# Encoder layer on one core: first gate weights loaded behind the first four x tiles, seven of the first head's weight subtractions on VectorE, two later norms issued one round sooner

## The chip, the cores and the metric

The kernel runs on one core of a Trainium2 chip. The metric is the device time of one execution in microseconds. Five engines matter here: TensorE (PE in the profile, with its weight loads as PEld), VectorE (DVE), ScalarE (ACT), GpSimd (POOL) and SyncE (SP), which issues most of the DMA transfers. Each engine executes its own instructions strictly in the order of its queue, and waits on semaphores where an instruction needs the result of another engine or of a transfer.

## What is computed

One residual encoder layer on x of 1024 positions by 1024 channels, in float32. Cut to what matters:

```python
h = rmsnorm(x, g_mix)
z = h @ w_in                      # columns: pooling channels | q | k | v
y_pool = pool_mixer(u_pool, w_pool_grp, pool_scale)
y_attn = diff_attention(q, k, v, g_q, g_k, lam, g_sub, lambda_init)   # 8 heads
gates = sigmoid(h @ w_gate + b_gate)
merged = gates[..., :1024] * (y_pool @ w_branch_pool) + gates[..., 1024:] * (y_attn @ w_branch_attn)
x = x + merged @ w_out
x = x + square(relu(rmsnorm(x, g_ffn) @ w_up)) @ w_down
```

## The kernel before

**Products.** A float32 operand is split into two parts: ScalarE copies it rounded (`hi`, a CAST row), and VectorE or GpSimd subtracts that from the source (`lo`, a TENSOR_TENSOR row). A product is then three matmuls into one PSUM bank, hi by hi, hi by lo and lo by hi (`mm3`, L138 to L140), so the third or the second of them waits for a subtraction. Weights and the normed, transposed h are both split in this way.

**The start of the program.** SyncE loads x0 (two halves), the first half of the first head's weights (`rqkv0_0`, `rqkv0_1`, each holding two of the eight k tiles), x1, the other half, two small rows, then x2 and x3. The list of instructions from there to the norm of x2 is written out by hand, and `q` (L423 to L432) chains every one of them behind the one before it on its engine, so that all of them carry the line L432. x0 and x1 are normed on ScalarE (Square with a sum), VectorE and GpSimd (a power of -0.5), scaled on VectorE (`hn`), transposed on TensorE into PSUM banks `hps`, and split into `hT`. `split_k(k)` splits weight tile k of the first head: ScalarE makes `hi`, and `POOL_W` lists the tiles whose `lo` GpSimd makes, VectorE making the others.

**The rounds.** After that a loop over rounds g issues stages of work for head h and position tile t (g = 8h + t): `A` is the q, k, v product `z` of one tile (24 matmuls of 384 columns into one of two PSUM banks of the pool `ps_z`), `B` its norm (`qn` on VectorE is the last reader of a `z` bank), `C` transposes q and k (`tk`), `D` the scores, and so on. x4 to x7 are loaded in rounds 0 and 1 (`LX`) and normed (`norm_x`, with `norm_transpose`, L282 and L287) in the rounds that `NX` lists. The norms of x1 to x7 there stand in `issue_after(h_hi[t - 2].ins)`: the norm's ScalarE instructions are queued behind the last `hi` copy of x(t-2). `issue_after` acts only on instructions of the engine of the one that it names.

**Fillers.** From round 5 on, half a unit a round, gate columns are computed between these stages: `gate_cols(c)` loads 128 columns of `w_gate` in two tiles (`frgate`, 256 KB each), splits them (`fwgate`, the subtraction on GpSimd) and multiplies them with the two halves of hT (`g`, 24 matmuls of 512 columns for each half of the positions).

**What sets the order.** The rounds give each instruction a priority; a scheduler then puts the instructions of each engine into a fixed order before the program runs, by its own estimate of when an operand is there. So an edit at one place can move instructions of all engines for some while after it. Here the order of all engines is the same again, row by row, from about the 1370th of TensorE's 7262 rows on.

Of the kernel before, what the change touches and what calls it, by code (L numbers as in the profile page):

```python
# [17 lines left out]
P = 128  # L18
# [19 lines left out]
N_QKVW = 8 * H  # L38


NX = [-9, -9, -9, -9, 2, 3, 3, 4]
LX = [-2, -2, -2, -2, 0, 0, 1, 1]
FU = 170
N_W1, N_W2 = 9, 16
POOL_W = (0,3,4,6)
G_DIST, G_COLS = 3, 2

O = "B1 C2 H7 D4 R8 E5 F6 W-2 A0"
# [15 lines left out]
def encoder_kernel(  # L64
# [21 lines left out]
    nc = tc.nc  # L86
    x, out = x[0], out[0]
# [69 lines left out]
    def fo_tile(name):  # L157
        return fp.tile([P, 528], F32, tag="fo", name=name, bufs=N_FO)
# [29 lines left out]
    loads = {}  # L188
# [103 lines left out]

    h_hi = {}

    def alloc_T(tile_fn, prefix, th):
        return {
            (kp, th, hl): tile_fn([P, 2, 512], F32R, f"{prefix}{kp}_{th}_{hl}", th)
            for kp in range(NK // 2)
            for hl in range(2)
        }  # L300
# [73 lines left out]
            nc.scalar.dma_start(p_dram[g * P : (g + 1) * P, th * 512 : (th + 1) * 512], yp[:, 0:512])  # L374

    def gate_cols(c):
        with tc.issue_after(h_hi[c + 2].ins) if c < 3 else nullcontext():
            ws = fill_w(w_gate, c * P, f"gate{c}")
        for th in range(2):
            ps = fill_proj(ws, th, f"g{c}_{th}", spare_bank if c >= G_Z else fill_bank)  # L380
            fo = fo_tile(f"go{c}_{th}")
            nc.scalar.activation(fo[:, 0:512], ps, AF.Identity, bias=cols[:, c : c + 1])  # L382
            nc.scalar.dma_start(g_dram[c * P : (c + 1) * P, th * 512 : (th + 1) * 512], fo[:, 0:512])
            yield
# [23 lines left out]
    with ExitStack() as ph:  # L408
# [8 lines left out]
        xs = {}  # L417
# [3 lines left out]
        @contextmanager  # L421
        def behind():
            with ExitStack() as stack:  # L423
                for ins in queued.values():
                    stack.enter_context(tc.issue_after(ins))
                yield

        def q(make, *args, **kw):
            if not in_turn[0]:
                return make(*args, **kw)  # L430
            with behind():
                done = make(*args, **kw)  # L432
            queued[done.ins.engine] = done.ins
            return done
# [9 lines left out]
        def load_x(t):  # L444
            xs[t] = htile([P, D], F32, f"x{t}", 1) if t < 2 else ut([P, D], F32, f"x{t}")
            for c in range(0, D, 512 if t < 2 else D):
                e = c + 512 if t < 2 else D
                q(nc.sync.dma_start, xs[t][:, c:e], x[t * P : (t + 1) * P, c:e])

        w_qkv = w_in[:, POOLD:].rearrange("(kk p) (s c) -> p kk s c", p=P, s=3)  # L450
        Wh = {}
# [94 lines left out]
        def turn(t, j):  # L546
            xt, hn, ss, s1_, rs = row[t]
            js = halves[j]
            if t == 0 and j == 0:
                q(act.activation, hn[:, js], hn[:, js], AF.Copy, scale=rs)  # L550
            else:
                q(dve.scalar_tensor_tensor, hn[:, js], xt[:, js], rs, gmb[:, js], op0=ALU.mult, op1=ALU.mult)
            pool_, tag = [(ps_t, "tr"), (ps_s, "sc")][j]
            ps = pool_.tile([P, 512], F32, tag=tag, name=f"hps{t}_{j}")
            for i in range(4):
                k = 4 * j + i
                go = q if t == 0 else lambda make, *args: make(*args)
                go(nc.tensor.transpose, ps[:, i * P : (i + 1) * P], hn[:, k * P : (k + 1) * P], identf)
            return ps
# [7 lines left out]
        def split_k(k, hi=True):  # L567
            if hi:
                Wh.setdefault(0, []).append(wt([P, 2, 384], f"wqkv0_{k}"))
            w, src = Wh[0][k], raws[0, k // 2][:, k % 2, :]  # L570
            if hi:
                q(act.copy, w[:, 0, :], src)
            if k or not hi:
                q((pol if k in POOL_W else dve).tensor_tensor, w[:, 1, :], src, f(w[:, 0, :]), op=ALU.subtract)

# [25 lines left out]
        split_h(0, 2, h0[1])  # L601
        scale_1()
        split_k(5)
        h1 = [turn(1, 0)]
        split_h(0, 3, h0[1])
        split_k(6)
        split_k(7)
        split_h(1, 0, h1[0])
        h1.append(turn(1, 1))
# [303 lines left out]
        for g in range(-2, N + 10):  # L913
            for t in range(4, NT):
                if LX[t] == g:
                    load_x(t)
            for t in range(1, NT):
                if NX[t] == g:
                    with tc.issue_after(h_hi[t - 2].ins):
                        norm_x(t)  # L920
            if g == G_DIST:
                with behind():
                    distances()
            if g == G_COLS:
                columns()
            gens = {}
            for tok in ORDER:
                if tok not in gens:
                    i = g - tok[1]
                    gens[tok] = stage(tok[0], i) if 0 <= i < N else iter(())  # L930
                next(gens[tok], None)
            for gen in gens.values():
                for _ in gen:
                    pass
            while made < F_UNITS and made < (g - F_FROM) * F_PACE:
                next(units)
                made += 1
# [82 lines left out]
    for d in range(NK):  # L1020
# [17 lines left out]
        if d >= 4:  # L1038
            e = d - 4
# [176 lines left out]
    for step in O_TAIL.split():  # L1216
        t = int(step[1])
# [396 lines left out]
```

## Time and profile before

| | us |
|---|---|
| median of three runs | 1532.42 (1532.18 to 1532.62) |
| the profiled execution's own time | 1534.07 |
| its span, first to last instruction | 1532.3 |
| TensorE busy in the span | 1518.9 |
| VectorE, ScalarE, GpSimd busy | 1023.4, 795.2, 393.9 |
| mean granted TensorE clock | 0.998 |

In a row of the timeline the first number is the start in us from the span's first instruction and the second the duration, then engine, source line, operation and tiles (buffer numbers left out), and in brackets the idle time of the engine before it with what ended that. "x4" is four such rows merged; "out<-in" names tiles by the program.

### The profile page before, as it was taken

The numbers are of one execution on the slowest core, as the hardware profiler recorded it, in microseconds if no ns is written. First come the engines' busy times: TensorE is split into PE (matmuls) and PEld (weight loads), VectorE is DVE, ScalarE is ACT, GpSimd is POOL, SyncE is SP. The second block draws the span as 40 slices with busy tenths as digits, with TensorE's granted clock in tenths as the row PEclk, the third lists the DMA queues.
The fourth block names the chain that finished last, engine by engine and source line by source line (L and its number), as shares of the span: only waits on it lengthen the run. The fifth ranks groups of instructions, "written<-read, shape, count | busy, mean of one in ns | idle before, by whom it ended". The sixth has DMA issues, their size and how long they took to land.

```text
span 1532.3 us, 21742 instructions
## 1 busy us (share of the span) xinstructions
PE 1518.9 (99%) x7637; PEld 1317.4 (86%) x7637; DVE 1023.4 (67%) x2132; ACT 795.2 (52%) x1653; POOL 393.9 (26%) x469
## 2 busy tenths in 40 slices
PE   8999999999999999999999999999999999999998
PEld 7899999999999999888888887888888788888887
DVE  7776767677777777742745898676656678556572
ACT  5755555555555555644633467565555634333331
POOL 5524242434334352318646510000000000000000
PEclk9999999999999999999999999999999999999999
DMA  6211111111202021339745633555433899537650
GB/s 211 64 38 58 47 56 56 58 49 40 73 30 80 30 90 49 117 104 375 266 141 185 203 135 117 172 183 167 152 124 110 289 328 365 186 125 261 230 189 28
DMA packets 168584, 213.75 MB, mean 139 GB/s; under 512 B 10166, under 2 KB 104091, under 8 KB 168475
## 3 DMA queue, kind: packets, MB, share of 16 engines
q1 hardware_dynamic: 151050, 185.05, 35.9%
q10 hardware_dynamic: 17424, 27.31, 4.8%
q8 instruction: 60, 0.98, 0.3%
q14 instruction: 50, 0.40, 0.1%
HBM read 154.62 MB, written 57.70 MB: 139 GB/s over the span
## 4 chain that ended last, share of the span: by engine, by line
PE 92%; DVE 5%; issue 1%; ACT 1%; DMA 0%; POOL 0%; POOLq 0%; SPq 0%; ACTq 0%; DVEq 0%
PE z L140 5%; PE z L139 5%; PE z L138 5%; PE Da L139 4%; PE Da L140 4%; PE g L139 4%; PE Da L138 4%; PE g L140 4%; PE g L138 4%; PE Db L140 3%; PE Db L139 3%; PE Db L138 3%; PE X L138 3%; PE X L140 3%; PE X L139 3%; PE sc L763 2%
## 5 line engine op out<-in xcount | busy, mean ns | idle before, releaser
L138 PE MATMUL z<-wqkv,hT 128*128 128x384 f32 x512 | 173.9, 340 | 0.3 <-DVE qn L699 0.3
L139 PE MATMUL z<-wqkv,hT 128*128 128x384 f32 x512 | 173.6, 339 | 0.5 <-POOL wqkv L432 0.5
L140 PE MATMUL z<-wqkv,hT 128*128 128x384 f32 x512 | 173.2, 339 | 0.2 <-DVE hT L430 0.2
L773 ACT ACTIVATE s<-s,nm 128x256 f32<-128x256 f32 (+7 forms) x128 | 99.6, 778 | 80.0 <-DVE nm L765 77.0
L271 POOL TENSOR_TENSOR ms<-ms,mhalf 128x4 f32<-128x4 f32 x64 | 66.9, 1045 | 200.1 <-DVE ms L270 196.6
L138 PE MATMUL g<-hT,fwgate 128*128 128x512 f32 x256 | 101.1, 395 | 0.0
L139 PE MATMUL g<-hT,fwgate 128*128 128x512 f32 x256 | 100.6, 393 | 0.2 <-DVE hT L132 0.2
L140 PE MATMUL g<-hT,fwgate 128*128 128x512 f32 x256 | 100.2, 392 | 0.0
L138 PEld LDWEIGHTS z<-wqkv,hT 128*128 128x128 f32 x512 | 96.2, 188 | 3.0 <-DVE qn L699 0.5
L139 PEld LDWEIGHTS z<-wqkv,hT 128*128 128x128 f32 x512 | 96.3, 188 | 2.7 <-POOL wqkv L432 0.8
L140 PEld LDWEIGHTS z<-wqkv,hT 128*128 128x128 f32 x512 | 96.2, 188 | 2.0 <-DVE hT L430 0.7
L765 DVE CUSTOM_DVE_ANT_0 s<-sc,dist 128x512 f32<-128x512 f32 (+3 forms) x128 | 74.4, 585 | 21.7 <-PE sc L763 21.0
L762 PE MATMUL sc<-K,Q 128*128 128x512 f32 (+2 forms) x192 | 67.6, 357 | 0.4 <-DVE nm L765 0.4
L763 PE MATMUL sc<-K,Q 128*128 128x512 f32 (+2 forms) x192 | 66.3, 349 | 0.0
L132 DVE TENSOR_TENSOR AS<-s,AS 128x512 fp32r<-128x512 f32 x64 | 43.5, 688 | 32.9 <-ACT AS L131 32.9
L132 POOL TENSOR_TENSOR wqkv<-rqkv,wqkv 128x384 fp32r<-128x384 f32 x56 | 58.6, 1059 | 13.7 <-ACT wqkv L131 12.2
L132 POOL TENSOR_TENSOR fwgate<-frgate,fwgate 128x512 fp32r<-128x512 f32 x32 | 43.6, 1366 | 58.6 <-ACT fwgate L131 58.6
L140 PEld LDWEIGHTS g<-hT,fwgate 128*128 128x128 f32 x256 | 48.1, 188 | 9.5
L139 PEld LDWEIGHTS g<-hT,fwgate 128*128 128x128 f32 x256 | 48.1, 188 | 9.3 <-DVE hT L132 0.6
L138 PEld LDWEIGHTS g<-hT,fwgate 128*128 128x128 f32 x256 | 48.1, 188 | 9.1 <-ACT go L382 0.2
L138 PE MATMUL ba<-yT,wba 128*128 128x512 f32 x128 | 49.6, 389 | 0.0
L139 PE MATMUL ba<-yT,wba 128*128 128x512 f32 x128 | 49.6, 389 | 0.0
(481 smaller groups left out, 4613.0 us busy)
## 6 DMA issues: line engine op xcount, KB each, us to landing
wd<-in_w_down_dram SPq DMA_DIRECT2D x56, 512.0 KB, 5.9
wu<-in_w_up_dram SPq DMA_DIRECT2D x32, 512.0 KB, 4.6
udS<-us SPq DMA_DIRECT2D x64, 256.0 KB, 3.5
ur<-udS SPq DMA_DIRECT2D x32, 512.0 KB, 4.4
rqkv<-in_w_in_dram SPq DMA_DIRECT2D x64, 192.0 KB, 3.4
ur<-ud SPq DMA_DIRECT2D x24, 512.0 KB, 6.0
frgate<-in_w_gate_dram SPq DMA_DIRECT2D x32, 256.0 KB, 2.7
g_dram<-go ACTq DMA_DIRECT2D x32, 256.0 KB, 3.0
```

The lines of the kernel that those rows point to most:

```text
L132: (lo_eng or nc.vector).tensor_tensor(lo, src, f(hi), op=ALU.subtract)
L138: nc.tensor.matmul(ps, lhs_hi, rhs_hi, start=first, stop=False, **kw)
L139: nc.tensor.matmul(ps, lhs_hi, rhs_lo, start=False, stop=False, **kw)
L140: return nc.tensor.matmul(ps, lhs_lo, rhs_hi, start=False, stop=last, **kw)
L271: nc.gpsimd.tensor_tensor(dst, dst, mhalf[:, :n], op=ALU.pow)
L762: nc.tensor.matmul(dst, Q[:, i, 0, :], rhs, start=True, stop=False)
L763: nc.tensor.matmul(dst, Q[:, i, 1, :], rhs, start=False, stop=True)
L765: nc.vector.tensor_tensor_reduce(out=s[i][:, c : c + w], in0=sc[:, 0:w], in1=dist[:, o0 + c : o0 + c + w], scale=2.0 ** -(h + 1), scalar=B ...
L773: nc.scalar.activation(s[i][:, 0:n], s[i][:, 0:n], AF.Exp, bias=last, scale=-1.0, accum_out=Z[:, i, t : t + 1])
```

## The change

Three things are edited. The loads of the first three gate columns get a second `issue_after`, behind the load of x3 on SyncE's queue; before, their only one named a ScalarE instruction and did not hold the loads. `POOL_W` shrinks from tiles 0, 3, 4, 6 to tile 3, and the split of weight tile 6 stands ahead of the scaling of x1 in the written list. The norms of x5 and x7 are issued in rounds 2 and 3 in place of 3 and 4, and the norms of x6 and x7 lose their `issue_after`.

```diff
-NX = [-9, -9, -9, -9, 2, 3, 3, 4]
+NX = [-9, -9, -9, -9, 2, 2, 3, 3]
-POOL_W = (0,3,4,6)
+POOL_W = (3,)
...
+    @contextmanager
+    def first_gates(c):
+        with tc.issue_after(h_hi[c + 2].ins), tc.issue_after(loads["x3"].ins):
+            yield
...
     def gate_cols(c):
-        with tc.issue_after(h_hi[c + 2].ins) if c < 3 else nullcontext():
+        with first_gates(c) if c < 3 else nullcontext():
...
-                q(nc.sync.dma_start, xs[t][:, c:e], x[t * P : (t + 1) * P, c:e])
+                loads[f"x{t}"] = q(nc.sync.dma_start, xs[t][:, c:e], x[t * P : (t + 1) * P, c:e])
...
         split_k(5)
+        split_k(6)
         h1 = [turn(1, 0)]
         split_h(0, 3, h0[1])
-        split_k(6)
         split_k(7)
...
-                    with tc.issue_after(h_hi[t - 2].ins):
+                    with tc.issue_after(h_hi[t - 2].ins) if t < 6 else nullcontext():
                         norm_x(t)
```

In the rows below the number behind a tile's name is its index in the program (`x0`, `hn5`, `frgate0_0`: first tile of gate column 0; `wqkv0_4`: head 0, weight tile 4; `z0_2`: head 0, position tile 2; `hps4_1`: second transposed half of x4; `g0_1`: gate column 0, second half of the positions), and the last number is a serial one. Source lines below L300 keep their numbers, later ones move by five.

SyncE, the first transfers that it issues, before:

```order
L307 DMA frgate0_0_789<-in_w_gate_dram 128x4x128
L432 DMA x0_145<-in_x_dram 128x512 x2
L432 DMA rqkv0_0_148<-in_w_in_dram 128x3x128 x2
L432 DMA rqkv0_1_151<-in_w_in_dram 128x3x128 x2
L432 DMA x1_154<-in_x_dram 128x512 x2
```

And the changed kernel's rows 13 to 18 of SyncE, behind x2, x3 and the small rows:

```order
L437 DMA rows_357<-in_g_sub_dram 1x128
L437 DMA rows_357<-in_g_ffn_dram 8x128
L437 DMA lqk_363<-in_lambda_qk_dram 128x256
L312 DMA frgate0_0_789<-in_w_gate_dram 128x4x128
L312 DMA frgate0_1_794<-in_w_gate_dram 128x4x128
L435 DMA rqkv1_0_850<-in_w_in_dram 128x3x128 x2
```

The first gate tile went from the head of the queue to the place just ahead of the second gate tile; the changed queue begins with x0.

VectorE, from the scaling of x0 to the sum of squares of x1, before:

```order
L432 SCALAR_TENSOR_TENSOR hn0_192<-x0_145,rsa0_195,gmb_179 128x512
L432 TENSOR_TENSOR wqkv0_1_246<-rqkv0_0_148,wqkv0_1_246 128x384
L432 TENSOR_TENSOR hT0_0_1_172<-hps0_0_234,hT0_0_0_171 128x2x128
L432 TENSOR_TENSOR wqkv0_2_251<-rqkv0_1_151,wqkv0_2_251 128x384
L432 TENSOR_TENSOR hT1_0_1_174<-hps0_0_234,hT1_0_0_173 128x2x128
L432 ISA hn1_262,ssb1_264<-x1_154 128x512
```

and now:

```order
L437 SCALAR_TENSOR_TENSOR hn0_192<-x0_145,rsa0_195,gmb_179 128x512
L437 TENSOR_TENSOR wqkv0_0_231<-rqkv0_0_148,wqkv0_0_231 128x384
L437 TENSOR_TENSOR wqkv0_1_246<-rqkv0_0_148,wqkv0_1_246 128x384
L437 TENSOR_TENSOR hT0_0_1_172<-hps0_0_234,hT0_0_0_171 128x2x128
L437 TENSOR_TENSOR wqkv0_2_251<-rqkv0_1_151,wqkv0_2_251 128x384
L437 TENSOR_TENSOR hT1_0_1_174<-hps0_0_234,hT1_0_0_173 128x2x128
L437 TENSOR_TENSOR wqkv0_4_259<-rqkv0_2_157,wqkv0_4_259 128x384
L437 ISA hn1_262,ssb1_264<-x1_154 128x512
```

Weight tiles 0 and 4 joined the queue here (and tile 6 further on, ahead of `hn1`).

VectorE again, ahead of `qn0_2`, the last reader of the PSUM bank that the product of position tile 4 takes next. Before:

```order
L695 TENSOR_REDUCE ms0_2_581<-sq0_2_580 128x4
L132 TENSOR_TENSOR V0_0_381<-z0_2_499,V0_0_381 128x128
L282 SCALAR_TENSOR_TENSOR hn5_524<-x5_375,rs5_526,gmb_179 128x512
L132 TENSOR_TENSOR hT0_1_1_451<-hps4_0_465,hT0_1_0_450 128x2x128
L282 SCALAR_TENSOR_TENSOR hn5_524<-x5_375,rs5_526,gmb_179 128x512
L270 TENSOR_SCALAR ms0_2_581<-ms0_2_581 128x4
L646 COPY cols_121<-cols_ps_484 128x32
L132 TENSOR_TENSOR hT1_1_1_453<-hps4_0_465,hT1_1_0_452 128x2x128
L647 TENSOR_SCALAR gs_122<-cols_121 128x1
L132 TENSOR_TENSOR hT2_1_1_455<-hps4_1_475,hT2_1_0_454 128x2x128
L132 TENSOR_TENSOR hT3_1_1_457<-hps4_1_475,hT3_1_0_456 128x2x128
L699 TENSOR_TENSOR qn0_2_588<-z0_2_499,ms0_2_581 128x256
```

and now:

```order
L700 TENSOR_REDUCE ms0_2_607<-sq0_2_606 128x4
L282 SCALAR_TENSOR_TENSOR hn5_484<-x5_375,rs5_486,gmb_179 128x512 x2
L132 TENSOR_TENSOR V0_0_381<-z0_2_525,V0_0_381 128x128
L132 TENSOR_TENSOR hT0_1_1_451<-hps4_0_465,hT0_1_0_450 128x2x128
L270 TENSOR_SCALAR ms0_2_607<-ms0_2_607 128x4
L282 SCALAR_TENSOR_TENSOR hn6_550<-x6_410,rs6_552,gmb_179 128x512 x2
L132 TENSOR_TENSOR hT1_1_1_453<-hps4_0_465,hT1_1_0_452 128x2x128
L700 TENSOR_REDUCE ms0_3_661<-sq0_3_660 128x4
L132 TENSOR_TENSOR V0_0_381<-z0_3_635,V0_0_381 128x128
L132 TENSOR_TENSOR hT2_1_1_455<-hps4_1_475,hT2_1_0_454 128x2x128
L270 TENSOR_SCALAR ms0_3_661<-ms0_3_661 128x4
L704 TENSOR_TENSOR qn0_2_614<-z0_2_525,ms0_2_607 128x256
```

Both halves of `hn6`, and two small steps of tile 3, now stand ahead of `qn0_2`. On ScalarE the Square of x6 likewise stands directly behind that of x5, ahead of the Square of `z0_2`.

TensorE, from the end of the product of tile 4 to the next work behind it. Before:

```order
L138 MATMUL z0_4_678<-wqkv0_7_286,hT3_1_0_456 128x384
L139 MATMUL z0_4_678<-wqkv0_7_286,hT3_1_0_456 128x384
L140 MATMUL z0_4_678<-wqkv0_7_286,hT3_1_1_457 128x384
L287 MATMUL hps7_1_651<-identf_95,hn7_634 128x128 x4
L138 MATMUL z0_5_755<-wqkv0_0_231,hT0_1_0_450 128x384
```

and now:

```order
L139 MATMUL z0_4_678<-wqkv0_7_286,hT3_1_0_456 128x384
L287 MATMUL hps7_0_583<-identf_95,hn7_576 128x128 x4
L140 MATMUL z0_4_678<-wqkv0_7_286,hT3_1_1_457 128x384
L287 MATMUL hps7_1_593<-identf_95,hn7_576 128x128 x4
L138 MATMUL g0_1_1016<-hT0_1_0_450,fwgate0_0_791 128x512
L725 MATMUL tk0_0_617<-identf_95,qn0_0_422 128x128 x2
L725 MATMUL tk0_0_617<-identf_95,qn0_1_522 128x128 x2
L139 MATMUL g0_1_1016<-hT0_1_1_451,fwgate0_0_791 128x512
```

Both transposes of x7 now come within the product of tile 4, and seven matmuls of the gate product `g0_1`, which needs the split columns of x7, stand ahead of `z0_5`.

## The prediction

> **What bounds the kernel now.** I read the busy times first, then the span cut into stretches (columns: the stretch, its length, busy time of PE, PEld, DVE, ACT and POOL, granted TensorE clock, share of the DMA engines, GB/s), then TensorE's waits, then the timeline at each wait.
>
> ```profile
> PE 1518.9 (99%) x7637; PEld 1317.4 (86%) x7637; DVE 1023.4 (67%) x2132; ACT 795.2 (52%) x1653; POOL 393.9 (26%) x469
> ...
> 0.00:9.00 9.00, 6.52 (x36) 6.07 (x36) 2.39 (x6) 4.19 (x8) 3.15 (x27) 1.00 0.73 230
> 9.00:18.00 9.00, 7.30 (x41) 6.00 (x42) 8.07 (x16) 5.73 (x18) 4.45 (x5) 1.00 0.97 312
> 30.00:41.00 11.00, 11.00 (x62) 9.61 (x61) 9.11 (x20) 5.82 (x16) 7.51 (x8) 1.00 0.33 96
> 41.00:56.00 15.00, 13.43 (x83) 12.21 (x81) 12.51 (x37) 9.88 (x28) 4.58 (x8) 1.00 0.05 19
> 56.00:330.00 274.00, 274.00 (x1600) 254.71 (x1599) 193.60 (x599) 158.58 (x413) 107.06 (x146) 1.00 0.18 56
> ...
> PE hps L432 <- ACT hn L432: 1.4, 1, 1.4
> ...
> PE hps L287 <- DVE hn L282: 1.1, 1, 1.1
> PE hps L557 <- DVE hn L432: 1.0, 1, 1.0
> ```
>
> TensorE is the bound: what changes neither its work nor its waits changes nothing. Its work is the same in both kernels, and its order is the same again from about 330 us on. From 56 to 330 us it is busy in all 274.00 us, so a gain can only come from the first 56 us: the wait for the first `hn` (1.4), and behind it five shorter ones, the two of 1.0 and 1.1 here and three whose rows follow.
>
> **Step 1, the gate tile behind the x tiles.**
>
> ```profile
> 0.74 0.43 SPq L307 DMA_DIRECT2D frgate<-in_w_gate_dram  x1
> 1.22 0.97 SPq L432 DMA_DIRECT2D x<-in_x_dram  x2
> ...
> 4.88 0.63 ACT L432 ACTIVATE hn<-x 128x512 f32<-128x512 f32 x1 [2.21 <-DMA x<-in_x_dram]
> 6.21 0.69 DVE L432 CUSTOM_DVE_ANT_0 hn<-x 128x512 f32<-128x512 f32 x1 [2.39 <-DMA x<-in_x_dram]
> 10.24 0.42 PE L138 MATMUL z<-wqkv,hT 128*128 128x384 f32 x1
> 13.09 0.40 SPq L307 DMA_DIRECT2D frgate<-in_w_gate_dram  x1
> 27.29 1.14 ACT L131 CAST fwgate<-frgate 128x512 fp32r<-128x512 f32 x2
> ```
>
> The first product starts at 10.24, at the end of a chain that begins when the second half of x0 lands (VectorE at 6.21, TensorE's wait of 1.4 in its middle). A gate tile of 256 KB is issued ahead of both halves. Without it x0 is issued 1.22 - 0.74 = 0.48 earlier, and that is the least. The most is the time between the two halves, also 256 KB each: 6.21 - 4.88 = 1.33. At the rates of the first two stretches 256 KB take 1.14 us (230 GB/s) or 0.84 (312). I take the middle, -0.95. Its new place costs nothing as far as the cover goes: the tile is first read at 27.29, and its twin, issued at 13.09, has 14 us already. SyncE's rows behind it (head 1's weights) move back by one issue of 0.40.
>
> **Step 2, weight tiles 0, 4 and 6 on VectorE.**
>
> ```profile
> 11.04 2.43 POOL L432 TENSOR_TENSOR wqkv<-rqkv,wqkv 128x384 fp32r<-128x384 f32 x2 [1.82 <-ACT wqkv L432]
> 14.27 1.00 POOL L432 TENSOR_TENSOR wqkv<-rqkv,wqkv 128x384 fp32r<-128x384 f32 x1
> ...
> 14.33 1.49 DVE L432 SCALAR_TENSOR_TENSOR hn<-x,rsa,gmb 128x512 f32<-128x512 f32 x1 [0.45 <-POOL rsa L432]
> 16.07 0.54 DVE L432 TENSOR_TENSOR wqkv<-rqkv,wqkv 128x384 fp32r<-128x384 f32 x1
> 17.31 0.74 DVE L432 SCALAR_TENSOR_TENSOR hn<-x,rsa,gmb 128x512 f32<-128x512 f32 x1
> ...
> 12.58 0.44 PE L138 MATMUL z<-wqkv,hT 128*128 128x384 f32 x1
> 13.52 0.45 PE L139 MATMUL z<-wqkv,hT 128*128 128x384 f32 x1 [0.50 <-POOL wqkv L432]
> 14.33 0.33 PE L140 MATMUL z<-wqkv,hT 128*128 128x384 f32 x1
> 14.50 0.34 PE L138 MATMUL z<-wqkv,hT 128*128 128x384 f32 x1
> 15.87 0.66 PE L557 MATMUL hps<-identf,hn 128*128 128x128 f32 x4 [1.03 <-DVE hn L432]
> ```
>
> Where nothing waits, these matmuls start 14.50 - 14.33 = 0.17 apart. From start to start, GpSimd's subtraction for tile 4 costs 13.52 - 12.58 - 0.17 = 0.77, and the late `hn1` 15.87 - 14.50 - 0.17 = 1.20. The first goes if VectorE has tile 4 ready by then. VectorE does three more subtractions of about 0.55: +1.65. What it gets back is the slowness beside GpSimd: the scaling takes 1.49 while GpSimd's row at 14.27 runs and 0.74 alone at 17.31, so 0.75 here, the same at `hn0`, and, as an estimate, 0.3 at each of two shorter rows, 2.1 together.
>
> The "GPSIMD Engine Reference" page of the Trainium skill (section 1, Specifications) says that GpSimd shares its SBUF interfaces with VectorE and contends with VectorE instructions of two SBUF inputs; the trace agrees (1.49 beside, 0.74 alone). By that sentence taken alone, with the 1.65 left out, `hn1` would come 2.1 sooner and both waits would go.
>
> The end of both waits is set by `hn1`, so the gain is how much sooner `hn1` is there: 2.1 - 1.65 = 0.45, and some 0.1 because the power ahead of it no longer queues behind GpSimd's pair at 11.04. I take -0.55: TensorE's waits in z of tile 0 and ahead of `hps1` come to about 1.4 in place of 1.97. Bounds: both vanish, -1.97; or GpSimd's cover is lost and half of the 1.65 comes on top, about +0.9.
>
> **Step 3, the norms a round sooner.**
>
> ```profile
> 39.69 0.42 DVE L699 TENSOR_TENSOR qn<-z,ms 128x256 f32<-128x256 f32 x1
> 40.76 0.33 PE L138 MATMUL z<-wqkv,hT 128*128 128x384 f32 x1
> ...
> 32.34 1.06 ACT L278 ACTIVATE hn<-x 128x1024 f32<-128x1024 f32 x1
> 28.25 3.46 DVE L282 SCALAR_TENSOR_TENSOR hn<-x,rs,gmb 128x512 f32<-128x512 f32 x2 [0.66 <-POOL rs L271]
> 45.95 1.42 DVE L282 SCALAR_TENSOR_TENSOR hn<-x,rs,gmb 128x512 f32<-128x512 f32 x2 [0.73 <-POOL rs L271]
> 46.11 0.34 PE L140 MATMUL z<-wqkv,hT 128*128 128x384 f32 x1
> 47.51 0.63 PE L287 MATMUL hps<-identf,hn 128*128 128x128 f32 x4 [1.06 <-DVE hn L282]
> 48.41 0.44 PE L138 MATMUL z<-wqkv,hT 128*128 128x384 f32 x1 [0.28 <-DVE qn L699]
> 53.60 0.40 PE L138 MATMUL g<-hT,fwgate 128*128 128x512 f32 x1
> 54.23 0.50 PE L139 MATMUL g<-hT,fwgate 128*128 128x512 f32 x1 [0.23 <-DVE hT L132]
> ```
>
> What goes, if x7's norm is done in time: 47.51 - 46.11 - 0.17 = 1.23; the wait for `qn` at 48.41, 0.28 idle and some 0.17 of start-up as in the others (1.06 idle cost 1.23), 0.45; and 54.23 - 53.60 - 0.23 = 0.40 (0.23 is one matmul of 512 columns). Together -2.08.
>
> What is late next. In the changed order `qn0_2` stands behind both scalings of x5 and x6, and ScalarE squares x5 and x6 back to back (1.06 each) ahead of the square of `z0_2`; so the last reader of the bank of `z0_2` moves back while TensorE, freed earlier, arrives sooner. Before, `qn0_2` ends at 40.11 and the product of tile 4 starts at 40.76, 0.65 of slack. With the 1.50 won so far TensorE could start at 39.26. I set `qn0_2` at 40.5 (0.95 sooner with the start, 1.06 later with the extra square, 0.3 for what VectorE has ahead of it): a new wait of 1.25. Bounds: 0, and 2.2 (without the start's 0.95). Behind it, x7's first `hT` is read seven matmuls sooner, by the gate product that now stands ahead of tile 5: half of 1.3 (the scaling of 1.42 late by nearly its length), 0.65; bounds 0 and 1.3.
>
> From 56 to 330 us there is no wait to win and one to make: GpSimd now makes gate 2's two subtractions ahead of head 1's weights: some 2.8 us, by the 2.12 of a pair of 384 columns below.
>
> ```profile
> 62.60 2.12 POOL L132 TENSOR_TENSOR wqkv<-rqkv,wqkv 128x384 fp32r<-128x384 f32 x2 [4.68 <-ACT wqkv L131]
> 71.10 0.33 PE L138 MATMUL z<-wqkv,hT 128*128 128x384 f32 x1
> ```
>
> Head 1's first two subtractions end at 64.72 and their product starts at 71.10, 6.4 of slack against the 2.8 put ahead of them, and the later tiles follow at GpSimd's pace. I put this at 0, bound +1.5.
>
> **Sum.** -0.95 - 0.55 - 2.08 + 1.25 + 0.65 = -1.68. The profiled execution took 1534.07 (its span 1532.3 and 1.77 outside it), 1.65 above the median of 1532.42. 1534.07 - 1.68 = 1532.39, or 1530.7 for the median. All ends the good way: -1.33 - 1.97 - 2.08 = -5.4, 1527.0; all the bad way, with the old waits gone: -0.48 + 0.9 - 2.08 + 2.2 + 1.3 + 1.5 = +3.3, 1535.7.
>
> **Rivals.**
>
> Faster: the two new waits at tile 4 and at the gate product do not come, since the later queue gets its rows done in the 11 us in which VectorE is busy only 9.11 of 11.00. Then -0.95 - 0.55 - 2.08 = -3.58, 1528.8. For it speaks the idle GpSimd; against it that VectorE is the fullest engine there beside TensorE.
>
> Slower: `qn0_2` is very late. Two scalings took 3.46 beside GpSimd's gate subtractions (28.25) and 1.42 alone (45.95), 2.04 more. In the changed kernel both pairs, x5's and x6's, stand ahead of `qn0_2`; if both meet gate subtractions, its wait grows by up to 4.1. From 1.25 + 1.68 = 2.9 us of wait on the kernel is slower; at both pairs it is -1.68 + 4.1 = +2.4, 1534.8.
>
> The start doesn't move: x0 waits for the memory and not for the gate tile's turn. Then only step 1 falls away: -0.73, 1531.7. Against it stands the DMA share of 0.73 in the first 9 us.
>
> The clock gives way.
>
> ```profile
> 936.00:940.00 4.00, 3.45 (x8) 2.57 (x9) 4.00 (x8) 2.92 (x6) 0.00 (x0) 0.64 0.92 267
> 938.41 0.63 PE L139 MATMUL Z<-BT1l,AS 128*128 128x512 f32 x1
> ```
>
> In these four us, behind waits of TensorE, the granted clock was 0.64; eight matmuls took 0.63 each there in place of 0.40 (the row at 53.60), some 0.2 longer from start to start, 1.6 us in all; after the waits before 56 us it stayed at 1.00. New waits that fall close together could bring such a stretch: -1.68 + 1.6 = -0.1, 1532.3. The page "TensorE: Matmul & The Clock Gate" of the Trainium skill (Part 1) gives a free-running window of about 3.4 us after whose idling the clock halves; the row at 936 agrees in length, and those at 14.50 and 46.11 only say that 1.2 us without a matmul did not suffice there.
>
> **How the numbers follow.** Forecast 0.42, no new waits 0.18, `qn0_2` very late 0.17, start unmoved 0.15, clock 0.08. The forecast's case gives 1530.7 and by itself reaches from 1529.3 to 1532.0 (each of its five terms off by some half of its way to a bound, not all to one side). The range takes in the rivals at 1528.8 and 1534.8: 1528.3 to 1534.8. A measurement of this kernel tells about 0.2% from no change, 3.1 us. Faster than 1529.4 are most of the second case and a tail of the first, 0.24; slower than 1535.5 only the worst part of the third with head 1's weights late as well, 0.13; within, 0.63.
>
> **What would show it.** Step 1: x0's second half lands at about 5.3 in place of 6.21, and the first product starts near 9.3. Step 2: no wait at weight tile 4, and waits of 1.4 in all up to `hps1`. Step 3: none of the waits at 46 to 54 us; in their place one for `qn` ahead of tile 4 (about 1.25) and one for `hT` at the gate product. From 56 us on, the two timelines at one constant distance. Wrong it would be if TensorE waits at head 1's first product, if the clock falls in the first 60 us, or if a wait of over 2.9 us stands ahead of tile 4.

## The result: 0.24% faster

The changed kernel takes 1529.82 us in the median of 16 runs (1528.89 to 1531.21), the kernel before 1533.15 (1532.18 to 1536.06). The ratio is 0.9976 with a 95% interval of 0.9968 to 0.9984, or 3.7 us less (2.5 to 4.9); the medians are 3.3 apart. The forecast was 1530.7 and 1.7 us less: the direction was the forecast's, and the size about half of what came. That the time itself came within 0.9 us is in part luck, since the kernel before has a median 0.7 us higher over its 16 runs than over the three runs that the forecast started from.

The profiled execution of the changed kernel has a span of 1526.9. Its busy times, then the stretches of the span (same columns as before), then TensorE's waits:

```profile
PE 1517.4 (99%) x7637; PEld 1316.2 (86%) x7637; DVE 1025.5 (67%) x2135; ACT 794.6 (52%) x1653; POOL 389.4 (26%) x466
```

```profile
0.00:9.00 9.00, 7.84 (x45) 7.36 (x45) 3.67 (x9) 5.13 (x10) 2.11 (x26) 1.00 0.75 228
9.00:18.00 9.00, 8.49 (x45) 6.68 (x46) 8.23 (x22) 6.45 (x18) 2.70 (x3) 1.00 0.99 312
...
30.00:41.00 11.00, 9.90 (x55) 8.56 (x54) 9.23 (x23) 7.76 (x19) 7.03 (x9) 1.00 0.25 72
41.00:56.00 15.00, 15.00 (x90) 13.88 (x89) 11.64 (x34) 9.84 (x30) 2.85 (x5) 1.00 0.05 19
56.00:330.00 274.00, 274.00 (x1606) 254.94 (x1605) 197.38 (x599) 158.04 (x412) 107.47 (x147) 1.00 0.18 57
```

```profile
PE z L138 <- ACT hT L131: 1.1, 1, 1.1
PE X L138 <- ACT BT2h L131: 0.8, 1, 0.8
PE Da L138 <- ACT w_0h L131: 0.7, 1, 0.7
```

TensorE is busy 7.84 and 8.49 of the first two nine-us stretches (before 6.52 and 7.30), all of 41 to 56 us (13.43 of 15.00 before), and in exchange it now idles 1.1 us between 30 and 41 us, where it had none. From 56 to 330 us nothing is idle in either kernel.

**Where the 5.4 us between the two profiled spans lie.** They are more than the 3.3 between the medians, for the profiled execution of the changed kernel is one of its fastest (1528.93) and that of the kernel before one of its slower ones (1534.07). I follow one TensorE instruction through both traces: the transposition ahead of the score product that waits for `nm`, in the long part in which both orders agree; below it is called the mark. It starts at 636.99 before and at 634.16 now: 2.83 us are won by then, and as TensorE has no idle time from 56 to 330 us and the orders agree from there on, they are won in the first 56. The other 2.5 us come later, out of code that did not change: 2.07 in the 60 matmuls from 931 us on, the rest nearly all behind the last matmul. The kernel before had there the stretch with the clock at 0.64 that the prediction showed; the changed kernel at the same instructions:

```profile
931.69 0.39 PE L138 MATMUL Z<-BT1h,AS 128*128 128x512 f32 x1
932.87 0.50 PE L138 MATMUL X<-BT2h,AS 128*128 128x512 f32 x1 [0.79 <-ACT BT2h L131]
934.04 0.40 PE L140 MATMUL Z<-BT1h,AS 128*128 128x512 f32 x1
```

```profile
934.58 0.39 PE L138 MATMUL Z<-BT1h,AS 128*128 128x512 f32 x1
936.22 0.49 PE L138 MATMUL X<-BT2h,AS 128*128 128x512 f32 x1 [1.25 <-ACT BT2h L131]
937.56 0.63 PE L140 MATMUL Z<-BT1h,AS 128*128 128x512 f32 x1
```

(The second fence is the kernel before.) Here TensorE idles 0.79 in place of 1.25, the clock stays up, and the matmuls take 0.40 and not 0.63.

One pair of traces is not enough for the split, though. A second trace of the changed kernel (`after_rep` in the table below) has the mark 0.61 later, at 634.77: ScalarE's Square of x4 waited 0.39 for its transfer there, at 24.93, and TensorE lost time behind it. The six traces that have all three steps and the changed order (two of this kernel, four of its variants below) lie between 634.16 and 634.77, so the first one is the earliest of them. Of the kernel as it was before there is one trace. So 2.2 to 2.8 of the runs' 3.3 to 3.7 us come from the start of the program, and 0.5 to 1.5 from waits late in it. Whether those belong to the change is what the last experiments ask.

**The start.** ScalarE, VectorE and TensorE of the changed kernel:

```profile
4.16 0.69 DVE L437 CUSTOM_DVE_ANT_0 hn<-x 128x512 f32<-128x512 f32 x1 [0.34 <-DMA x<-in_x_dram]
5.24 0.58 ACT L437 COPY gmb<-gb 128x512 f32<-128x512 f32 x1 [1.02 <-PE gb L437]
5.85 0.69 DVE L437 TENSOR_TENSOR hn<-x,gmb 128x512 f32<-128x512 f32 x1 [0.66 <-ACT gmb L437]
6.79 0.75 DVE L437 SCALAR_TENSOR_TENSOR hn<-x,rsa,gmb 128x512 f32<-128x512 f32 x1 [0.25 <-ACT gmb L437]
...
5.71 2.30 PE L437 MATMUL warm<-ones 128*128 128x256 f32 x16
7.85 1.03 PE L437 MATMUL hps<-identf,hn 128*128 128x128 f32 x8
8.91 0.44 PE L138 MATMUL z<-wqkv,hT 128*128 128x384 f32 x1
12.20 0.45 PE L140 MATMUL z<-wqkv,hT 128*128 128x384 f32 x1 [0.28 <-DVE hT L437]
13.99 0.66 PE L562 MATMUL hps<-identf,hn 128*128 128x128 f32 x4 [0.24 <-DVE hn L437]
```

The second half of x0 lands 2.05 us sooner (VectorE starts on it at 4.16 against 6.21), well beyond the bound of 1.33. In all ten traces with the load moved VectorE starts on it at 4.07 to 4.90, in the four others at 6.21 to 6.99. But the first product gains 1.33 (8.91 against 10.24): VectorE now waits 0.66 and 0.25 for ScalarE's copies of the norm vector `gmb`, which wait for TensorE's broadcast `gb`, and the transposes start right behind the last warm-up matmul. The scaling takes 0.75, with no GpSimd subtraction beside it. x1's transposes start at 13.99 against 15.87, 1.88 sooner.

**The new order at 40 us.**

```profile
38.29 0.40 PE L140 MATMUL g<-hT,fwgate 128*128 128x512 f32 x1
38.70 0.21 PE L650 MATMUL cols_ps<-identf,rows 32*128 32x32 f32 x1
40.00 0.41 PE L138 MATMUL z<-wqkv,hT 128*128 128x384 f32 x1 [1.08 <-ACT hT L131]
...
39.44 0.41 DVE L704 TENSOR_TENSOR qn<-z,ms 128x256 f32<-128x256 f32 x1
...
46.08 0.51 PE L138 MATMUL g<-hT,fwgate 128*128 128x512 f32 x1
46.78 0.48 PE L139 MATMUL g<-hT,fwgate 128*128 128x512 f32 x1
```

The new wait ahead of tile 4 is there, 1.08 idle; it is put down to a `hT` copy on ScalarE that ends at the same time as `qn0_2` (39.44 + 0.41 = 39.85). The product waits for both, and both hang on x6's scalings: the copy itself had waited 2.05 for a VectorE subtraction that, like `qn0_2`, stands behind them in VectorE's queue. The three waits at 46 to 54 us are gone, and the gate product has no wait for x7's `hT`: its second row follows four transposes.

### The profile page after: what moved, and what is told of

It reads as the page before. It is cut to its first block, busy times and chain, and to the rows that moved or that the text cites. A ratio compares the mean times of both kernels' runs of the same rounds, so it can differ in the third digit from the quotient of the medians.

```text
span 1526.9 us, 21743 instructions
## 1 busy us (share of the span) xinstructions
PE 1517.4 (99%) x7637; PEld 1316.2 (86%) x7637; DVE 1025.5 (67%) x2135; ACT 794.6 (52%) x1653; POOL 389.4 (26%) x466
## 4 chain that ended last, share of the span: by engine, by line
PE 96%; DVE 2%; DMA 1%; ACT 1%; issue 0%; SPq 0%; POOLq 0%; POOL 0%; ACTq 0%; DVEq 0%
PE z L138 6%; PE z L139 5%; PE z L140 5%; PE Da L139 4%; PE Da L140 4%; PE Da L138 4%; PE g L138 4%; PE g L139 4%; PE g L140 4%; PE Db L138 3%; PE Db L139 3%; PE Db L140 3%; PE X L138 3%; PE X L139 3%; PE X L140 3%; PE sc L767 2%
## 5 line engine op out<-in xcount | busy, mean ns | idle before, releaser
L132 DVE TENSOR_TENSOR AT_0l<-ta,AT_0h 128x512 fp32r<-128x512 f32 (+1 forms) x48 | 32.0, 666 | 32.0 <-ACT AT_0h L131 31.7
L139 PE MATMUL ba<-yT,wba 128*128 128x512 f32 x128 | 49.6, 389 | 0.0
```

Of the source, the lines that this page charges most:

```text
L132: (lo_eng or nc.vector).tensor_tensor(lo, src, f(hi), op=ALU.subtract)
L139: nc.tensor.matmul(ps, lhs_hi, rhs_lo, start=False, stop=False, **kw)
```

## The experiments

The table has, of the profiled execution of each kernel, the start of the first product, of x1's transposes and of the marked transposition near 635 us, and the length of two stretches of 60 matmuls, from 931 and from 1217 us. Between these places, and from there to the last matmul, the kernels agree within 0.1 us, but for 1.2 us near 905 in `b_both` and 0.16 in `before_w8`. Each row is one execution, and the two of the changed kernel differ by 0.6 at the mark; so a smaller difference of marks counts only where the rows at the place of the edit account for it. The last columns are the median and the ratio to the kernel before on the same chip (median there 1533.14, 1533.24 and 1533.01 in the three sets).

| | first product | x1 | mark | from 931 | from 1217 | median | ratio (95%) |
|---|---|---|---|---|---|---|---|
| before | 10.24 | 15.87 | 636.99 | 18.12 | 14.99 | 1533.15 | |
| changed | 8.91 | 13.99 | 634.16 | 16.05 | 14.93 | 1529.82 | 0.9976 (0.9968 to 0.9984) |
| s1_loads | 9.37 | 15.05 | 636.20 | 16.07 | 17.37 | 1532.10 | 0.9990 (0.9981 to 0.9999) |
| s2_subs | 10.27 | 15.35 | 636.35 | 18.18 | 15.37 | 1532.66 | 0.9995 (0.9987 to 1.0004) |
| s3_norms | 10.40 | 16.04 | 636.26 | 16.14 | 15.19 | 1532.17 | 0.9992 (0.9983 to 1.0001) |
| s12 | 8.90 | 14.28 | 635.30 | 16.38 | 14.92 | 1531.17 | 0.9984 (0.9975 to 0.9993) |
| b_nx6 | 8.89 | 13.96 | 634.77 | 16.05 | 15.03 | 1529.85 | 0.9977 (0.9968 to 0.9986) |
| b_warm8 | 8.74 | 14.11 | 634.26 | 16.66 | 18.01 | 1531.60 | 0.9986 (0.9977 to 0.9995) |
| b_start | 8.54 | 14.11 | 634.30 | 16.55 | 15.65 | 1531.92 | 0.9993 (0.9984 to 1.0002) |
| b_both | 8.54 | 14.94 | 635.69 | 16.87 | 14.90 | 1532.47 | 0.9995 (0.9986 to 1.0004) |
| after_rep | 8.69 | 14.09 | 634.77 | 16.33 | 15.17 | 1529.76 | 0.9976 (0.9966 to 0.9986) |
| warm8_rep | 8.89 | 14.01 | 634.18 | 18.25 | 17.90 | 1532.04 | 0.9992 (0.9983 to 1.0001) |
| after_w15 | 9.43 | 14.50 | 634.68 | 18.09 | 15.37 | 1530.46 | 0.9983 (0.9975 to 0.9992) |
| before_w8 | 11.46 | 17.10 | 638.18 | 16.51 | 18.01 | 1533.67 | 1.0008 (0.9999 to 1.0017) |

### Each step alone

`s1_loads`, the changed kernel with everything but the load's second condition put back:

```diff
-NX = [-9, -9, -9, -9, 2, 2, 3, 3]
+NX = [-9, -9, -9, -9, 2, 3, 3, 4]
-POOL_W = (3,)
+POOL_W = (0,3,4,6)
...
-        split_k(6)
         h1 = [turn(1, 0)]
         split_h(0, 3, h0[1])
+        split_k(6)
...
-                    with tc.issue_after(h_hi[t - 2].ins) if t < 6 else nullcontext():
+                    with tc.issue_after(h_hi[t - 2].ins):
```

> Step 1 alone (the gate tile behind the x tiles). Theory, each step acts at its own place and nothing behind it takes the gain back: the second half of x0 lands about 2.0 us sooner (near 4.2), the first product starts between 0.9 and 1.3 sooner than 10.24, its end held by GpSimd's weight tile 0 and the slow scaling beside it; TensorE stays that far ahead to the end, so -0.9 to -1.3 us in time. Rival, the start of the changed kernel needs both steps: step 1 alone brings under 0.5 us, since the scaling of x0 beside GpSimd still ends late.

```profile
5.71 2.76 PE L437 MATMUL warm<-ones 128*128 128x256 f32 x16
8.31 1.03 PE L437 MATMUL hps<-identf,hn 128*128 128x128 f32 x8
9.37 0.44 PE L138 MATMUL z<-wqkv,hT 128*128 128x384 f32 x1
12.70 0.44 PE L139 MATMUL z<-wqkv,hT 128*128 128x384 f32 x1 [0.49 <-POOL wqkv L437]
15.05 0.66 PE L562 MATMUL hps<-identf,hn 128*128 128x128 f32 x4 [1.02 <-DVE hn L437]
```

The first product is 0.87 sooner, a little under the expected 0.9, the mark 0.79, the median 1.0. The two waits that step 2 removes (0.49, 1.02) stand as before. The gain isn't lost behind; the rival falls.

That 0.87 came and not the 1.33 of the whole change is not for want of steps 2 and 3. ScalarE's scaled half of x0 is there at 7.71 in both traces, but the warm-up matmuls ahead of the transposes end later here (2.76 in place of 2.30): they start 0.21 us apart until 7.11 and 0.12 from there on, in the changed kernel's trace 0.12 apart from 6.07 on. The first clock record, from which the granted clock is 1.00, lies at 7.05 and 6.05 in these two, and from 4.95 to 7.50 in the 14 traces. So with 16 warm-up matmuls the start now ends with them, and at a time that differs from execution to execution. The kernel before had slack there: TensorE idled 1.41 between its last warm-up matmul and the first transposes.

`s2_subs`, the subtractions alone:

```diff
-NX = [-9, -9, -9, -9, 2, 2, 3, 3]
+NX = [-9, -9, -9, -9, 2, 3, 3, 4]
...
-        with first_gates(c) if c < 3 else nullcontext():
+        with tc.issue_after(h_hi[c + 2].ins) if c < 3 else nullcontext():
...
-                    with tc.issue_after(h_hi[t - 2].ins) if t < 6 else nullcontext():
+                    with tc.issue_after(h_hi[t - 2].ins):
```

> Step 2 alone (weight tiles 0, 4 and 6 on VectorE). Theory: the scaling of x0 takes 0.75 in place of 1.48, x0 lands as before (6.21), and the end of the transposes of x1's first half comes 0.5 to 0.9 sooner than 15.87: -0.5 to -0.9 us. Rival, step 2 pays only behind an earlier start: within 0.3 us of before, as VectorE's three added subtractions (1.65 us) stand in the way of hT.

```profile
8.38 0.75 DVE L437 SCALAR_TENSOR_TENSOR hn<-x,rsa,gmb 128x512 f32<-128x512 f32 x1 [0.45 <-POOL rsa L437]
13.56 0.44 PE L140 MATMUL z<-wqkv,hT 128*128 128x384 f32 x1 [0.28 <-DVE hT L437]
15.35 0.66 PE L562 MATMUL hps<-identf,hn 128*128 128x128 f32 x4 [0.24 <-DVE hn L437]
```

The scaling takes 0.75 in place of 1.48, x1's transposes start 0.52 sooner, the mark 0.64; by the runs 0.5, with an interval that holds zero, so the times alone don't show it. What does is the time from the first product to x1's transposes: 5.63 to 5.68 in the four traces without step 2, and 5.07 to 5.12 in five of the ten with it. In the other five (5.37 to 6.40) ScalarE's copies of the weights ran late: in four of them the copy of weight tile 4 waited 0.42 to 0.97 for its transfer, and `b_start` had put a copy of the norm vector ahead of it. So the rival (nothing without step 1) falls by the trace. Part of the gain does not reach the time: device time less span is 2.21 us here in the median, 1.79 for the kernel before and 1.99 for the changed one; why, the runs don't show.

`s3_norms`, the norms alone:

```diff
-POOL_W = (3,)
+POOL_W = (0,3,4,6)
...
-        with first_gates(c) if c < 3 else nullcontext():
+        with tc.issue_after(h_hi[c + 2].ins) if c < 3 else nullcontext():
...
-        split_k(6)
         h1 = [turn(1, 0)]
         split_h(0, 3, h0[1])
+        split_k(6)
```

> Step 3 alone (the norms a round sooner). Theory, the new wait ahead of tile 4's product comes from the new order and not from TensorE's lead: about 1.1 us of idle there as in the changed kernel, the waits at 46 to 54 us (2.08) gone, -1.0 us in all. Rival, the wait comes from TensorE's being sooner by the 1.9 us of steps 1 and 2: no wait of over 0.3 us there, and -1.8 to -2.1 us.

```profile
42.10 0.41 PE L138 MATMUL z<-wqkv,hT 128*128 128x384 f32 x1 [1.09 <-ACT hT L131]
...
41.54 0.41 DVE L704 TENSOR_TENSOR qn<-z,ms 128x256 f32<-128x256 f32 x1
```

The wait ahead of tile 4 is 1.09 here as well, without the lead of steps 1 and 2 (1.08 with it). It is 1.08 or 1.09 in all seven traces with this order. So the order makes it, and `qn0_2` moves with the start as TensorE does. The median is 1.0 lower, with an interval that just holds zero. The mark is 0.73 sooner, 0.9 if x0's later landing in this execution (VectorE's first row at 6.39 against 6.21, with the loads unchanged) is taken off.

`s12`, steps 1 and 2: `NX` and the norms' `issue_after` as before.

> Steps 1 and 2 without step 3. Theory, the steps add: -1.9 us, with the first product at 8.9 and the waits at 46 to 54 us all back (1.2, 0.4, 0.4), each shifted by 1.9. Rival, VectorE's and GpSimd's queues are looser there after an earlier start, and part of these waits (over 0.5 us of 2.08) goes without step 3: -2.4 us or more.

The first product starts at 8.90 and the mark is 1.69 sooner, the median 2.0. The waits at 45 to 52 us are back at 1.16, 0.44 and 0.41. Together: marks 0.79 + 0.64 + 0.73 = 2.16 for the three alone against 2.83 for the change; with x0's landing taken off (0.09 in s2, 0.18 in s3) 2.43. By the medians 1.0 + 0.5 + 1.0 = 2.5 against 3.3. The three alone fall 0.4 to 0.8 short of the change, which is no more than two executions of one kernel differ at the mark and less than the intervals of the medians: as far as these runs can tell, they add.

### Can the remaining waits go?

`b_nx6` puts x6's norm behind the `hi` copies of x4 again, so that `qn0_2` stands ahead of x6's scalings on VectorE:

```diff
-                    with tc.issue_after(h_hi[t - 2].ins) if t < 6 else nullcontext():
+                    with tc.issue_after(h_hi[t - 2].ins) if t < 7 else nullcontext():
```

> The changed kernel, with x6's norm again behind the hi copies of x4 (one half of step 3's second edit undone); qn0_2 then stands ahead of both scalings of x6 on VectorE. Theory, the wait of 1.1 us ahead of tile 4's product is made by x6's scalings in front of qn0_2: it falls to under 0.2, and as x6 and x7 come later in exchange, 0.3 to 1.0 comes back at their transposes inside tile 4: -0.1 to -0.8 us against the changed kernel, 2.9 to 3.9 against the kernel before. Rival, the wait only moves: the transposes of x6 and x7 wait 1.1 us or more between them, and the time is within 0.2 us of the changed kernel or above it.

```profile
37.55 0.41 DVE L704 TENSOR_TENSOR qn<-z,ms 128x256 f32<-128x256 f32 x1
...
38.89 0.34 PE L138 MATMUL z<-wqkv,hT 128*128 128x384 f32 x1
45.16 0.63 PE L287 MATMUL hps<-identf,hn 128*128 128x128 f32 x4 [0.37 <-DVE hT L132]
46.35 0.63 PE L725 MATMUL tk<-identf,qn 128*128 128x128 f32 x4 [0.56 <-DVE hT L132]
```

`qn0_2` is 1.9 sooner and tile 4 starts at 38.89 without a wait: x6's norm ahead of it was the cause. (The edit also moves x6's Square on ScalarE back behind the Square of `z0_2`; the two are not separated.) But behind tile 4 TensorE then waits from start to start 0.23, 0.53, 0.73 and 0.29 for the later norms, 1.8 in all. The mark is 0.6 later than in the changed kernel's first trace and level with its second, the medians are level. The rival holds: the wait moves.

`b_warm8` has 8 warm-up matmuls ahead of the first transposes, and `b_start` moreover reads the norm vector from PSUM, makes its second copy later, and makes the copy of weight tile 0 ahead of the second scaling:

```diff
-N_W1, N_W2 = 9, 16
+N_W1, N_W2 = 9, 8
```

```diff
-                q(dve.tensor_tensor, hn[:, 0:512], xt[:, 0:512], gmb[:, 0:512], op=ALU.mult)
+                q(dve.tensor_tensor, hn[:, 0:512], xt[:, 0:512], gbs[0], op=ALU.mult)
...
-                q(dve.scalar_tensor_tensor, hn[:, js], xt[:, js], rs, gmb[:, js], op0=ALU.mult, op1=ALU.mult)
+                q(dve.scalar_tensor_tensor, hn[:, js], xt[:, js], rs, gmb[:, js] if t else gbs[j], op0=ALU.mult, op1=ALU.mult)
...
-            q(act.copy, gmb[:, halves[j]], gb)
+            gbs.append(gb)
+        q(act.copy, gmb[:, halves[0]], gbs[0])
...
+        h0 = [turn(0, 0)]
         split_k(0)
-        h0 = [turn(0, j) for j in range(2)]
+        h0.append(turn(0, 1))
...
         split_h(0, 0, h0[0])
+        q(act.copy, gmb[:, halves[1]], gbs[1])
```

> The changed kernel with 8 in place of 16 warm-up matmuls ahead of the first transposes. In the changed kernel these follow the last warm-up matmul at once (7.85). If the warm-up is now the end of the start, the first product comes up to 0.2 us sooner (ScalarE's scaled half is there at 7.72), not more. If the norm vector's copies (5.24 and 6.09 on ScalarE, behind TensorE's broadcast) hold the start, nothing moves but that 0.1 to 0.2; if the clock falls for want of warm-up, the first products take up to twice as long and 1 us or more is lost.

> The changed kernel with 8 warm-up matmuls, and with x0's two products reading the broadcast norm vector from PSUM instead of from ScalarE's copies, the second copy being made later. Theory, since step 1 let x0 land at 4.2 the start is held by that vector: VectorE's product of x0 then starts at about 5.2 in place of 5.85, the first transposes at about 6.9 in place of 7.85 and the first product 0.7 to 1.0 sooner than 8.91; the time 0.5 to 1.0 us below the changed kernel. Rival, the loads of the weights are next: the first weight tiles land no sooner than before, the copies of the later ones wait for transfers, and less than 0.3 us is left by the transposes of x1.

Three rows of `b_warm8` and then two of `b_start`:

```profile
7.63 1.09 PE L437 MATMUL hps<-identf,hn 128*128 128x128 f32 x8 [0.76 <-ACT hn L437]
10.21 0.51 ACT L437 CAST wqkv<-rqkv 128x384 fp32r<-128x384 f32 x1 [0.42 <-DMA rqkv<-in_w_in_dram]
11.66 0.44 PE L138 MATMUL z<-wqkv,hT 128*128 128x384 f32 x1 [0.38 <-ACT hT L437]
```

```profile
5.86 0.69 DVE L437 TENSOR_TENSOR hn<-x,gb 128x512 f32<-128x512 f32 x1 [0.60 <-ACT gmb L437]
8.54 0.45 PE L138 MATMUL z<-wqkv,hT 128*128 128x384 f32 x1
```

The first product comes 0.17 and 0.37 sooner, x1's transposes 0.12 later. With 8 warm-up matmuls the transposes wait 0.76 for ScalarE's half, so the warm-up no longer holds them; the first product takes its usual 0.44, so the clock did not fall there. But the gain is no more than executions differ by: the changed kernel's second trace has 8.69 and 14.09. The copy of weight tile 4 waits 0.42 for its transfer in `b_warm8`; it waited 0.46 in that second trace as well, with 16 warm-up matmuls. In `b_start` the wait is 0.14, and the copy of the norm vector that the edit moved (0.59) stands ahead of it on ScalarE. `b_start` does not test its theory: VectorE's product of x0 starts at 5.86 as before, and its row still waits for ScalarE's copy, although it no longer reads it. The edit did not free it, and why that wait is in the program stays open. Of the rival, that nothing is left by x1's transposes holds, and that the weights are next is seen in some executions. Up to the mark both kernels are level with the changed one (634.26 and 634.30 against 634.16), and yet their medians are 1.8 and 2.1 higher.

`b_both` is `b_start` with the order of `b_nx6`.

> Both together, the start of b_start and the order of b_nx6. If the two act at different places they add: 0.6 to 1.8 us below the changed kernel, 3.5 to 5.3 below the kernel before. If TensorE's larger lead at 38 us only makes the wait ahead of tile 4 longer again, no more than the better one of the two.

It is the slowest of the four, 1532.47: in the traced execution ScalarE waited 0.97 for weight tile 4's transfer, and the waits of `b_nx6` are all there. Nothing adds.

### The late waits

Why do kernels that are level at 635 us differ by 2 us? Two kernels were run again and two with other warm-up counts beside them: `after_rep` is the changed kernel, `warm8_rep` is `b_warm8`, `after_w15` has `N_W2 = 15`, and `before_w8` is the kernel before with `N_W2 = 8`.

> The changed kernel once more. What is asked: 2.84 us of its gain stand in the traces by 637 us, and the kernel with 8 warm-up matmuls, level with it there (0.1 apart), ran 1.8 us longer in the median. Theory A, the waits at 930 and 1217 us differ from program to program as loaded: this one again 3.0 to 3.9 us below the kernel before, and the one with 8 warm-up matmuls again 1.3 to 2.3 above this. Theory B, they differ from execution to execution only: over two sets of runs the two medians come within 0.7 us of each other.

> The changed kernel with 8 warm-up matmuls once more. Theory A: 1.3 to 2.3 us above the changed kernel in the same set, the extra in the waits at 930 and 1217 us. Theory B: within 0.7 us of it.

> The changed kernel with 15 warm-up matmuls, the least edit of the start: by the trace the first product may come 0.1 us sooner. Theory A: its time may lie up to 2 us from the changed kernel's although everything up to 637 us is level within 0.3. Theory B, and any theory in which only the first 57 us count: within 0.5 us.

> The kernel before with 8 warm-up matmuls. There TensorE waits 1.4 us for the first hn behind its 16 warm-up matmuls, so that the first product starts at 10.24 with 8 as well (within 0.2). Theory A: the time may lie up to 2 us from the kernel before. Theory B: the same within 0.5 us. If fewer warm-up matmuls themselves cost later time, this one is slower by 1.3 to 2.3 as the changed kernel was.

The two medians of the changed kernel are 1529.82 and 1529.76, the two with 8 warm-up matmuls 1531.60 and 1532.04: each repeats, 1.8 and 2.3 apart. Theory B, chance between executions, falls. The traces put the difference into the two late waits (18.01 and 17.90 from 1217 us against 14.93 and 15.17). In the changed kernel's traces TensorE waits 0.7 and 0.9 there (0.7 quoted above), with 8 warm-up matmuls 2.5 and 2.4 (here `b_warm8`):

```profile
PE Da L138 <- ACT w_0h L131: 2.5, 1, 2.5
PE X L138 <- ACT BT2h L131: 1.4, 1, 1.4
```

and behind it the clock falls (stretch from 1219 us of the same execution):

```profile
1219.00:1225.00 6.00, 4.54 (x13) 3.59 (x14) 4.25 (x6) 6.00 (x10) 0.00 (x0) 0.72 0.61 226
```

What the two waits hang on stands in ScalarE's queue: `w_0h` comes behind `u_2h`, which waits for a transfer back from DRAM. That row in the changed kernel and in `b_warm8`:

```profile
1212.17 1.05 ACT L131 CAST u_2h<-ur 128x1024 fp32r<-128x1024 f32 x1 [2.17 <-DMA ur<-ud]
```

```profile
1214.76 1.05 ACT L131 CAST u_2h<-ur 128x1024 fp32r<-128x1024 f32 x1 [2.53 <-DMA ur<-ud]
```

It is 2.6 later, where TensorE is 0.75 later. Why the transfers of one program come later than those of another with the same order there is not settled: `b_start` and `b_both` also have 8 warm-up matmuls and waited only 1.4 and 0.6 there in their traces, and `before_w8` is 0.7 above its base by the medians. Theory A in its plain form, an effect of the program as loaded, fits the repeats; no cause was found.

`after_w15` decides nothing: its median is 0.7 above that of `after_rep`, outside the 0.5 of theory B, but the intervals reach 1.3 us to either side. Its first product came 0.5 later (9.43) and not 0.1 sooner: the clock record that ends the slow warm-up came at 7.50.

`before_w8` missed its first point as well. Its first product starts at 11.46 and not at 10.24:

```profile
9.84 1.97 PE L432 MATMUL hps<-identf,hn 128*128 128x128 f32 x8 [2.91 <-ACT hn L432]
11.46 0.67 PE L138 MATMUL z<-wqkv,hT 128*128 128x384 f32 x1
```

x0 landed 0.78 later in that execution (6.99), and after 2.91 us without work TensorE ran its eight transposes in 1.97 and a product in 0.67, against 1.42 and 0.42; the granted clock is 0.50 from 9.20 to 12.61.

## Why the prediction was right, step by step

**What bounds the kernel.** Right: everything that is shown to come from the change lies in the first 56 us, and the stretch from 56 to 330 us stayed at 274.00 of 274.00. Head 1's product did not wait.

**Step 1, -0.95.** Mis-sized: the first product came 1.33 sooner in the change, and 0.87 in the trace of the load alone, where the clock rose later. The bound of 1.33 was wrong: x0's second half landed 2.05 sooner. The prediction took the issue (0.48) and the transfer (at most 1.33) one against the other, and together they are still short of it by 0.24; why, the runs don't show. That only 1.33 of it arrived was due to waits that the prediction did not name, for the norm vector's copies on ScalarE and then for the warm-up matmuls on TensorE.

**Step 2, -0.55.** Right, and that it is right to the digit is luck: x1's transposes are 1.88 sooner in all, 1.33 by the first product and 0.55 behind it; alone 0.52. In `after_rep` and `s12`, where weight tile 4 came late, only 0.23 and 0.25 arrive. The reason was right also: the scaling fell from 1.49 to 0.75 once GpSimd no longer subtracts beside it. The waits on the way came to less than the forecast's 1.4 (0.44 and 0.40 from start to start, 0.28 and 0.24 of it idle), but some 0.4 more went into starts a little further apart and 0.17 into one product more ahead of the transposes, so that the end came out as forecast.

**Step 3, -2.08 and +1.25 and +0.65.** The three waits went, as forecast. The wait ahead of tile 4 came, and near the forecast size: 40.00 - 38.70 is 1.30 from start to start, 1.13 without the usual 0.17. Its cause was read rightly (b_nx6 takes it away by moving `qn0_2` ahead of x6's scalings), but part of the reason was wrong: it does not grow with TensorE's lead (1.09 without it). The term that failed is +0.65 for x7's first `hT`: the gate product did not wait. x7's scalings ran at 42.42, ahead of the gate product at 46.08, so `hT` was there in time, and the bound's lower end, 0, was the value.

**The sum.** -1.68 forecast; by the mark of the first trace -2.83. Of the 1.15 between, 0.65 is the gate product's wait that did not come, 0.38 is step 1, and 0.12 the wait ahead of tile 4; in the second trace 0.61 of this is lost again, by a later start of x4's norm. The runs show 0.5 to 1.5 more than the marks, in waits at 930 and 1217 us that were in no term; the changed kernel's short late waits repeat over two sets of runs, but kernels with the same order there differ by as much, so this part is not shown to be an effect of the three steps.

**The rivals.** "No new waits" (1528.8) was half true: one came, one did not. "qn0_2 very late" fell: VectorE's x5 scalings met a GpSimd subtraction (2.51 for the pair), x6's did not (1.41), and the wait was 1.1. "The start doesn't move" fell: x0 lands 2.05 us sooner. The clock rival did not happen in the first 60 us; it was late in the program that it moved the time, and there in favour of the change. Its page, "TensorE: Matmul & The Clock Gate" of the Trainium skill (Part 1), speaks of a free-running window of about 3.4 us, after whose idling the clock halves. The traces agree on the window: a half-clock stretch inside the program lasts 3.41 us and begins a whole multiple of 3.413 us behind the first clock record (in the kernel before at 937.15, 931.84 or 273 times 3.413 behind the one at 5.31). They show besides that the window need not be idle throughout. Two rows of the kernel before and two of `b_both` (columns as above: TensorE's busy time stands behind the length, the granted clock third from the end):

```profile
933.74:937.15 3.41, 1.83 (x8) 0.98 (x7) 3.41 (x7) 3.41 (x7) 0.00 (x0) 1.00 0.72 220
937.15:940.56 3.41, 3.41 (x9) 2.63 (x10) 3.41 (x7) 1.76 (x4) 0.00 (x0) 0.50 0.97 287
935.30:938.71 3.41, 1.93 (x7) 1.39 (x8) 3.41 (x7) 2.98 (x7) 0.00 (x0) 1.00 0.82 266
938.71:942.12 3.41, 3.41 (x17) 2.81 (x16) 3.41 (x7) 2.70 (x6) 0.00 (x0) 1.00 0.94 324
```

I divided all 14 traces into such windows. Up to the last matmul, TensorE was busy 1.85 us or less in the nine windows ahead of a half-clock stretch, and 1.93 or more in all others; only in the window that holds the last matmul did 1.58 and 1.70 pass without one. So the length of one wait does not decide: at 930 us waits of 1.41 to 1.51 us from start to start (less the usual 0.23) were followed by half clock in four traces (before, s2_subs, after_w15, warm8_rep), and of 1.41, 1.43, 1.54 and 1.77 in four others they were not, where the idle time was split between two windows.

## What to carry to other kernels

Where one engine is busy all the time but for a few short waits, a change of the order is worth the sum of those waits that go less those that come, and each can be sized from the rows around it (here three of five terms came within 0.15 us in the first trace, the others missed by 0.4 and 0.65); what moves behind the next reader of a PSUM bank is the thing to look for. A load that isn't needed soon belongs behind those that are, and the gain stops at the next late operand (here the norm vector, the warm-up matmuls, and in some executions the weights), so the second-latest arrival bounds it. Against differences of 0.1 to 0.2%, first compare one marked instruction in both traces, and in two traces of the same kernel: a median can hold 1 to 2 us from a late stage that the change never touched, and the mark itself moved by 0.6 from one execution to the next.

## What the runs showed that I had not expected

- The warm-up matmuls run at half pace until the first clock record, which came anywhere from 4.95 to 7.50 us; once x0 is early, this moves the first product from 8.69 to 9.43 in six traces with 15 or 16 of them. With 8 it is 8.54 to 8.89, but in `before_w8`, with x0 late and 2.91 us idle, eight transposes then took 1.97 in place of 1.42.
- Kernels with the same instruction order after 330 us had late waits that differ by up to 3 us (14.90 to 18.01 for 60 matmuls), and where a kernel was run again, its median repeated within 0.06 us (the changed kernel) and 0.44 (8 warm-up matmuls). The cause is open.
- A half-clock stretch of 3.41 us costs about 1.6 us (2.07 between the two traces from 931 us on, less 0.46 of longer wait), and the share of executions whose mean granted clock was under 1.000 differs: 4 of 25 for the changed kernel, 42 of 97 for the kernel before, 15 of 22 for `b_warm8` and its repeat.
